# Both gates' first 512 columns computed as one Strassen unit of seven block products between the q and k products

## The chip, the cores and the metric

The kernel runs on one core of a Trainium2 chip. Its time is the device time of one launch in microseconds (us), the median of several runs. The engines are TensorE (PE: matmul, with PEld for its weight loads), VectorE (DVE), ScalarE (ACT), GpSimd (POOL) and SyncE (SP), which issues most transfers. On-chip data lies in SBUF, and matmuls write to banks of PSUM.

## The reference

Two layers, each with a feed-forward part, a mixer and a second feed-forward part, with layer norms between them. There are 256 tokens and 1024 channels, all in float32. The change is in the mixer:

```python
def _mixer(x, layer, w_in, gate_b, ...):
    z = x @ w_in                                   # 256 x 1024 times 1024 x 7168
    u, v, q, k, val, gates = jnp.split(z, SPLITS, axis=-1)
    ...
    q = _rope(q, cos, sin)                         # rotary
    k = _rope(k, cos, sin)
    o = _diff_attention(q, k, val, lam_full)       # 8 heads
    ...
    g = jax.nn.sigmoid(gates.reshape(bsz, seq, N_BRANCH, D_MODEL) + gate_b)
    m = g[:, :, 0] * (h_a @ w_branch[0]) + g[:, :, 1] * (h_b @ w_branch[1])
    return m @ w_out
```

`gates` is x times 2048 columns: 1024 for each of the two branches. The change is about the first 512 columns of each branch, so a product of 256 x 1024 with 1024 x 1024.

## The kernel before, in words

Float32 products are made of three matmuls. Each weight is split into a high part (`hi`, ScalarE, `activation Copy`, lines 195 and 247) and a low part (`lo`, VectorE, a subtraction, lines 197 and 249), x likewise, and a product is hi by hi, lo by hi and hi by lo. A weight arrives as a tile `raw` of 128 x 2048 floats, 1 MB, by a transfer that SP issues (`fetch`, line 173). Four such tiles are there, and eight halves each of `hi` and `lo`. So weights are fetched and split up to four tiles ahead of TensorE. A new fetch into a `raw` waits until VectorE has made the low parts of its old content.

Two forms of product stand in the mixer. `gemm_a2` takes weights as the stationary side: 16 matmuls of 128x512 (line 295) and 16 of 128x256 (line 302). ScalarE copies one half of the bank to `r` (line 303) and VectorE adds the other half into z (lines 305, 307). `gemm_b` takes x as the stationary side, with matmuls of 128x512 in line 283. `product`, with its matmul in line 376, is one block of a Strassen product as the feed-forward parts use them: 12 matmuls of 128x512. `gather` (line 353) adds a second weight onto a `raw` in place, by two accumulating transfers of 512 KB that GpSimd issues. `pieces` splits a raw into its high and low halves. `strassen_sums` makes four sums of blocks of x on VectorE and splits them.

The order on TensorE is the order of the code. The other engines' instructions are ordered ahead of the run by a scheduler that takes the code's order as priority. `beat` counts TensorE's work in units of 12 matmuls of 128x512. `beside(task, n)` lets a task's steps run n such units later, among the products. `behind(ins)` keeps an instruction behind another one on its engine.

A mixer runs as follows:

- `val`, two column blocks by `gemm_b2`.
- Four pairs of heads `hp`. For each a q product and a k product by `rope`, which multiplies z with the cosine on VectorE (line 992), swaps halves of z by two transfers on SP (line 989), multiplies the swapped half with the sine on GpSimd (line 993) and adds both on VectorE (line 997). Then `attend(hp)` as a task, 4.5 + 2.1 hp units later: scores (line 1017), masked copies with maxima on VectorE (line 1029), exponentials on ScalarE (line 1031), the difference of both maps on VectorE (lines 1048, 1049, 1040), copies on GpSimd (line 216), transposing transfers on SP (line 220), and the product with `val` (lines 1071, 1073).
- For each branch `gate_rows`, 48 matmuls in line 283 for 512 gate columns with VectorE's addition of the bias (line 1125) and a tanh on ScalarE, and `gate_columns`, two `gemm_a2` for the other 512 columns.
- Then u, v, the branch products, the output product and the norm.

`Norm` computes a layer norm in pieces and leaves x and its transposed blocks `rows`; the norm with `front` 0 is the one ahead of a mixer.

Of the kernel before, what the change touches and what calls it, by code (L numbers as in the profile page):

```python
# [17 lines left out]
ALU = mybir.AluOpType  # L18
# [36 lines left out]
def trunk(ctx, tc, x, xT, w13a, w13b, w2, wb, wqk, wu, wg, wgr, wbr, wbrr, wo, gateb, gatebr, sgug, sgub, sguwT, sgubias, lam, diffg,  # L55
# [538 lines left out]
    class Norm:  # L594
# [25 lines left out]

        def halved(self):
            with behind(line[0]):
                A.activation(self.g, self.g, AF.Copy, scale=-0.5)
            yield 0
# [30 lines left out]
        def finish(self, t, waits):  # L655
# [3 lines left out]
            if not self.last:  # L659
                r = rsqrt(mv[:, 1:2], self.eps)  # L660
                halves = slice(0, 512), slice(512, D)
                if t:
                    self.via += [t512("nvia") for _ in halves]
# [7 lines left out]
                if t == 0:  # L671
                    self.via.append(s512("nvia"))
# [36 lines left out]
        def turned(self, wait):  # L709
# [5 lines left out]
            self.affine(0, 0, b, s512("xf"), (4,))  # L715
# [59 lines left out]
        def close(self):  # L775
# [3 lines left out]
            return self  # L779

    def ffn(l, f, i, norm, last=False):
# [77 lines left out]

        def strassen_sums(to, made, v11, v21, v12, v22, apart=1, after=lambda: None):  # L860
            to[:] = [tuple(lambda k, v=v: v[:, k * P : (k + 1) * P] for v in m) for m in made]
            for n, (out, a, b, op) in ((0, (v22, v21, v22, ALU.subtract)), (2, (v21, v11, v21, ALU.subtract)),
                                       (1, (v11, v22, v11, ALU.subtract)), (3, (v12, v12, v11, ALU.add))):
                with behind(after()):
                    V.tensor_tensor(out=out, in0=a, in1=b, op=op)
                if n in (2, 3):
                    yield apart
            for n, out in ((0, v22), (2, v21), (1, v11), (3, v12)):
                split(*(v if len(out.shape) == 2 else v.rearrange("p (k t) -> p k t", k=4) for v in made[n]), out)
                yield apart  # L870
# [98 lines left out]
    def mixer(l, i, norm):  # L969
# [139 lines left out]

        for hp in range(HEADS // 2):  # L1110
            qT = rope(wqk[l, hp, 0], HD ** -0.5)
            kT = rope(wqk[l, hp, 1], 1.0)
            beside(attend(hp, qT, kT), 4.5 + 2.1 * hp)
            if hp == 1:
                gbias = bc_load(gatebr[l], qT[:, :1])

        gates, grow = [], []

        def gate_rows(br):

            gr = [slots("gr", 2)[0] for _ in range(NT)]
            grow.append(gr)

            def done(t, ps, c, n):
                added[0] = V.tensor_tensor(out=gr[t], in0=ps, in1=gbias[:, br * 512 : (br + 1) * 512], op=ALU.add).ins
                emptied[0] = A.activation(gr[t], gr[t], AF.Tanh, scale=0.5).ins
# [231 lines left out]
```

## Time and profile before

| what | value |
|---|---|
| median of 3 runs | 1186.49 us (1186.29 to 1186.53) |
| span of the profiled execution | 1185.1 us |
| granted clock of TensorE | 1.000 |
| HBM read | 248.05 MB, 210 GB/s over the span |
| longest instruction group of VectorE | line 197, 346 times, 379.4 us |

The span is that of one execution under the profiler, from its first to its last instruction; the runs' times also hold what lies around it. Busy time of an engine is a sum over stages, so a stage is read from windows of it, and what an engine waited for from the waits. In a row of a timeline the first number is the start, the second the duration, and x the count of instructions joined in it; neighbours on one engine overlap a little, so costs are taken from start to start. Layer 0's q product begins at 202.44 us on TensorE, layer 1's at 788.67 us.

### The profile page before, as it was taken

The page shows a single profiled execution, that of the slowest core. Times are in us where ns is not written, and L with a number is a line of the kernel's source. Part 1 is how long each engine was busy: PE and PEld are TensorE (multiplying, and loading weights), DVE is VectorE, ACT ScalarE, POOL GpSimd, SP SyncE. Part 2 cuts the span into 40 slices and gives each one's busy share as a digit, 9 for nine tenths or more (in the row PEclk, how much of TensorE's full clock was granted, in tenths as well). Part 3 has the DMA queues.
Part 4 walks back from the last instruction along what each step waited for, and adds up shares of the span by engine and source line. Part 5 has one row for each costly group of instructions (what it writes and reads, how often), then busy time and mean ns, then how long its engine had stood idle before and what let it go on. Part 6 is the DMA issues. An engine that isn't in the chain of part 4 may idle for free.

```text
span 1185.1 us, 16676 instructions
## 1 busy us (share of the span) xinstructions
PE 1180.5 (100%) x5777; PEld 995.0 (84%) x5777; DVE 1013.1 (85%) x1562; ACT 828.1 (70%) x1419; POOL 287.5 (24%) x350
## 2 busy tenths in 40 slices
PE   9999999999999999999999999999999999999998
PEld 8888888888888888888888888888888888888887
DVE  6989989788688989889899889888965989988895
ACT  6688658559955677876667876576788556679761
POOL 1011201247420220051020161003564112102600
PEclk9999999999999999999999999999999999999999
DMA  9869976767865658699668689586666755786881
GB/s 355 265 198 262 287 273 208 266 193 238 246 205 173 227 188 273 187 275 267 239 220 265 190 278 280 198 290 232 212 204 208 250 181 174 247 254 208 273 260 36
DMA packets 129621, 275.10 MB, mean 232 GB/s; under 512 B 89041, under 2 KB 90369, under 8 KB 105473
## 3 DMA queue, kind: packets, MB, share of 16 engines
q1 hardware_dynamic: 121968, 248.67, 63.5%
q0 software_dynamic: 6992, 24.71, 8.7%
q8 instruction: 45, 0.74, 0.2%
q10 hardware_dynamic: 576, 0.66, 0.2%
q14 instruction: 40, 0.32, 0.1%
HBM read 248.05 MB, written 1.05 MB: 210 GB/s over the span
## 4 chain that ended last, share of the span: by engine, by line
PE 99%; DVE 0%; DVEq 0%; issue 0%
PE bank L283 46%; PE bank L295 15%; PE sbank L376 12%; PE bank L410 10%; PE bank L302 8%; PE sbank L410 3%; PE bank L530 2%; PE sbank L1017 1%; PE bank L376 1%; PE sbank L1073 1%; PE sbank L1191 1%; PE sbank L542 0%; PE sbank L1071 0%; PE sbank L714 0%; DVE xtok L701 0%; DVE st L643 0%
## 5 line engine op out<-in xcount | busy, mean ns | idle before, releaser
L197 DVE TENSOR_TENSOR wlo<-raw,whi 128x1024 fp32r<-128x1024 f32 (+1 forms) x346 | 379.4, 1123 | 51.8 <-ACT whi L195 38.0
L195 ACT ACTIVATE whi<-raw 128x1024 fp32r<-128x1024 f32 (+1 forms) x350 | 323.4, 952 | 135.1 <-PE bank L283 43.0
L283 PE MATMUL bank<-whi,x 128*128 128x512 f32 x1224 | 386.4, 390 | 0.0
L283 PEld LDWEIGHTS bank<-whi,x 128*128 128x128 f32 x1224 | 229.8, 188 | 47.8
L283 PE MATMUL bank<-wlo,x 128*128 128x512 f32 x612 | 238.2, 389 | 0.0
L249 DVE TENSOR_TENSOR wlo<-raw,whi 128x1024 fp32r<-128x1024 f32 (+1 forms) x123 | 142.9, 1185 | 20.3 <-ACT whi L247 11.4
L247 ACT ACTIVATE whi<-raw 128x1024 fp32r<-128x1024 f32 (+1 forms) x123 | 121.1, 1003 | 51.2 <-DVE raw L359 23.9
L295 PE MATMUL bank<-x,whi 128*128 128x512 f32 x640 | 153.3, 391 | 0.0
L295 PEld LDWEIGHTS bank<-x,whi 128*128 128x128 f32 x640 | 118.2, 188 | 23.8
L283 PEld LDWEIGHTS bank<-wlo,x 128*128 128x128 f32 x612 | 114.9, 188 | 23.1
L229 POOL COPY seven<-seven 128x512 uint16<-128x512 uint16 x16 | 58.8, 3733 | 135.2 <-ACT whi L195 54.6
L302 PEld LDWEIGHTS bank<-x,wlo 128*128 128x128 f32 x640 | 81.4, 191 | 2.9
L302 PE MATMUL bank<-x,wlo 128*128 128x256 f32 x640 | 82.6, 283 | 0.0
L410 PE MATMUL bank<-whi,hhi 128*128 128x512 f32 (+1 forms) x182 | 68.2, 374 | 0.0
L410 PE MATMUL bank<-whi,hlo 128*128 128x512 f32 (+1 forms) x182 | 67.9, 373 | 0.0
L410 PE MATMUL bank<-wlo,hhi 128*128 128x512 f32 (+1 forms) x182 | 67.9, 373 | 0.0
L993 POOL TENSOR_TENSOR swap<-swap,sin_t 128x512 f32<-128x512 f32 x16 | 26.9, 1680 | 101.2 <-DMA swap<-z 84.4
L757 POOL COPY nvia<-ntwo 128x256 uint16<-128x256 uint16 x20 | 10.0, 547 | 161.2 <-DMA ntwo<-nvia 148.2
L303 ACT ACTIVATE r<-bank 128x256 f32<-128x256 f32 x96 | 34.9, 373 | 16.3 <-PE bank L302 16.1
L376 PE MATMUL sbank<-whi,xhs 128*128 128x512 f32 x128 | 42.0, 389 | 0.0
L410 PEld LDWEIGHTS bank<-whi,hlo 128*128 128x128 f32 x182 | 34.3, 188 | 6.0
L410 PEld LDWEIGHTS bank<-whi,hhi 128*128 128x128 f32 x182 | 34.3, 188 | 6.0
(292 smaller groups left out, 2157.6 us busy)
## 6 DMA issues: line engine op xcount, KB each, us to landing
raw<-in_w13b SPq DMA_DIRECT2D x68, 1024.0 KB, 6.0
raw<-in_w SPq DMA_DIRECT2D x32, 1024.0 KB, 7.0
raw<-in_wb SPq DMA_DIRECT2D x16, 1024.0 KB, 6.7
raw<-in_wqk SPq DMA_DIRECT2D x16, 1024.0 KB, 6.2
home<-in_w13b SPq DMA_DIRECT2D x16, 512.0 KB, 5.9
raw<-in_w13a SPq DMA_DIRECT2D x8, 1024.0 KB, 4.9
home<-in_w SPq DMA_DIRECT2D x16, 512.0 KB, 4.9
raw<-in_wgr SPq DMA_DIRECT2D x8, 1024.0 KB, 5.4
```

What stands on the lines that cost most here:

```text
L195: inline(A, A.activation(h, r, AF.Copy).ins)
L197: low = eng.tensor_tensor(out=w, in0=r, in1=h.bitcast(F32), op=ALU.subtract).ins
L229: eng.tensor_copy(out=o, in_=i)
L247: a = A.activation(hi, src, AF.Copy).ins
L249: return a, eng.tensor_tensor(out=lo, in0=src, in1=hi.bitcast(F32), op=ALU.subtract).ins
L283: PE.matmul(ps, xx, w, start=start and n == 0, stop=stop and n == 2)
L295: PE.matmul(b[-1], hi[:, k * P : (k + 1) * P], xc(k), start=k == 0, stop=False)
L302: PE.matmul(b[n][:, :T], lo[:, k * P : (k + 1) * P], xc(k)[:, :T], start=False, stop=k == KT - 1)
L303: emptied[0] = A.activation(r[:, s], b[n][:, T:], AF.Copy, scale=scale).ins
L376: PE.matmul(ps, x[o](k), y, start=start and k == n == 0, stop=stop and k == 3 and n == 2, skip_group_check=True)
L410: PE.matmul(q[c][t][:, :n] if o == 0 else more[:, :n], x(k, t), y, start=k == 8 and m == 0 and (c, t) != (1, 0) and not o, stop=k == FT - ...
L993: turned_by[0] = G.tensor_tensor(out=s3, in0=s3, in1=s, op=ALU.mult).ins
```

## The change

Both branches' first 512 columns become one 2 x 2 block product: x in blocks of 128 tokens by 512 channels, weights in blocks of 512 channels by 512 columns, one column block for each branch. It is computed by seven block products P1 to P7 of 12 matmuls each in place of 96 matmuls. The blocks' weights w11, w21 and w22 are fetched; w12, and the sums that follow, come in by `gather`: r1 holds w11, then w11 + w12, then with w22 added, then with w21 added, and r3 holds w22, then w22 + w12. The bank `bz` serves P3 and P4, `bx` serves P1, P5, P6 and P7; VectorE copies the intermediate values out between. The four sums of x (`strassen_sums`, now outside `ffn`) are made by a task 2.5 units behind the start of the q and k products, into eight slots `xhs`.

The generator `gates_by_rows` is advanced by `next(products)`: behind k0 for P1, behind q1 for P2, and so on, so that TensorE has q0 k0 P1 q1 P2 k1 P3 q2 P4 k2 P5 q3 P6 k3 P7. An attend comes 4.5 + 0.1 hp units after its k. The gate bias is loaded ahead of the q products. The norm ahead of the mixer keeps some tiles in slots and no longer in temporary tiles (`home`), since they are read longer.

```diff
--- before.py
+++ after.py
@@ -618,6 +618,9 @@
                 self.via = []
                 self.x = [xs.tile([P, 4, 512], F32R, tag="x", name=name("x")) for _ in range(2)]
 
+        def home(self, s, other):
+            return other(s) if self.front else slots(s, 2)[0]
+
         def halved(self):
             with behind(line[0]):
                 A.activation(self.g, self.g, AF.Copy, scale=-0.5)
@@ -660,7 +663,7 @@
                 r = rsqrt(mv[:, 1:2], self.eps)
                 halves = slice(0, 512), slice(512, D)
                 if t:
-                    self.via += [t512("nvia") for _ in halves]
+                    self.via += [self.home("nvia", t512) for _ in halves]
                 for h in (0, 1) if t else (1, 0):
                     s = halves[h]
                     with behind(self.ends[t]):
@@ -669,7 +672,7 @@
                     if t:
                         self.ends[t] = self.plane(V, t, h, 1)
                 if t == 0:
-                    self.via.append(s512("nvia"))
+                    self.via.append(self.home("nvia", s512))
                     for w in range(2):
                         self.ends[t] = self.plane(V, 0, 1, w)
                     beside(self.turned(waits), 0)
@@ -712,7 +715,7 @@
             b = side_bank()
             for k in range(4):
                 PE.transpose(b[:, k * P : (k + 1) * P], self.y[0][:, k * P : (k + 1) * P], ident)
-            self.affine(0, 0, b, s512("xf"), (4,))
+            self.affine(0, 0, b, self.home("xf", s512), (4,))
             yield 9
             yield from self.tokens(0)
 
@@ -778,6 +781,18 @@
                 x_cat = self.x
             return self
 
+    def strassen_sums(to, made, v11, v21, v12, v22, apart=1, after=lambda: None):
+        to[:] = [tuple(lambda k, v=v: v[:, k * P : (k + 1) * P] for v in m) for m in made]
+        for n, (out, a, b, op) in ((0, (v22, v21, v22, ALU.subtract)), (2, (v21, v11, v21, ALU.subtract)),
+                                   (1, (v11, v22, v11, ALU.subtract)), (3, (v12, v12, v11, ALU.add))):
+            with behind(after()):
+                V.tensor_tensor(out=out, in0=a, in1=b, op=op)
+            if n in (2, 3):
+                yield apart
+        for n, out in ((0, v22), (2, v21), (1, v11), (3, v12)):
+            split(*(v if len(out.shape) == 2 else v.rearrange("p (k t) -> p k t", k=4) for v in made[n]), out)
+            yield apart
+
     def ffn(l, f, i, norm, last=False):
         xh, xl = parts(both)
         h_hi, h_lo = ([act.tile([P, 512], F32R, tag="slot", name=name(n)) for _ in range(FT // 2)] for n in ("hhi", "hlo"))
@@ -856,18 +871,6 @@
 
             made = [[home(v) for v in w] for w in (("main", "side"), ("side", "main"), ("main", "slot"), ("side", "slot"))]
             yield from strassen_sums(x_sums, made, t11, t21, t12, t22, after=lambda: None if norm else line[1])
-
-        def strassen_sums(to, made, v11, v21, v12, v22, apart=1, after=lambda: None):
...
 
         def seven(src, x_sums):
 
@@ -1107,25 +1110,68 @@
                     V.scalar_tensor_tensor(out=lo, in0=f, scalar=dl, in1=hi.bitcast(F32), op0=ALU.mult,
                                             op1=ALU.subtract)
 
+        gates, x_sums = [], []
+        grow = [[slots("gr", 2)[0] for _ in range(NT)] for _ in range(2)]
+        gbias = bc_load(gatebr[l], val[1][:, 1, :1])
+
+        def sums_of_x():
+            made = [slots("xhs", 4, F32R) for _ in range(4)]
+            t11, t12, t21, t22 = (norm.rows[v] for v in ((0, 0), (0, 1), (1, 0), (1, 1)))
+            yield from strassen_sums(x_sums, made, t11, t21, t12, t22, after=lambda: added[0])
+
+        def gates_by_rows():
+
+            x11, x12, x22 = (tuple(lambda k, o=o, t=t, h=h: x_cat[h][:, k, o + t * P : o + (t + 1) * P] for o in (0, T))
+                             for t, h in ((0, 0), (0, 1), (1, 1)))
+            (w11, w21), (w12, w22) = ([wgr[l, br, 0][:, o : o + CH] for o in (0, CH)] for br in range(2))
+            (g00, g10), (g01, g11) = grow
+            bias = [gbias[:, br * 512 : (br + 1) * 512] for br in range(2)]
+
+            def sum_up(out, in0, in1, op, end=False):
+                added[0] = V.tensor_tensor(out=out, in0=in0, in1=in1, op=op).ins
+                if end:
+                    emptied[0] = A.activation(out, out, AF.Tanh, scale=0.5).ins
+
+            bx = bank()
+            r1 = fetch(w11)
+            product(bx, x11, pieces(r1), True, False)
+            gather(r1, w12)
+            sum_up(g00, bx, bias[0], ALU.add)
+            yield
+            bq = bank()
+            product(bq, x12, pieces(fetch(w21)), True, True)
+            sum_up(g00, bq, g00, ALU.add, True)
+            yield
+            bz = bank()
+            product(bz, x_sums[0], pieces(r1), True, False)
+            gather(r1, w22)
+            sum_up(g11, bz, bias[1], ALU.add)
+            yield
+            r3 = fetch(w22)
+            product(bz, x_sums[3], pieces(r3), False, True)
+            gather(r3, w12)
+            sum_up(g01, bz, bias[1], ALU.add)
+            yield
+            product(bx, x_sums[1], pieces(r1), False, False)
+            gather(r1, w21)
+            sum_up(g01, g01, bx, ALU.subtract, True)
+            yield
+            product(bx, x_sums[2], pieces(r3), False, False)
+            sum_up(g11, g11, bx, ALU.subtract, True)
+            yield
+            product(bx, x22, pieces(r1), False, True)
+            sum_up(g10, bx, bias[0], ALU.add, True)
+            yield
+
+        products = gates_by_rows()
+        beside(sums_of_x(), 2.5)
         for hp in range(HEADS // 2):
             qT = rope(wqk[l, hp, 0], HD ** -0.5)
+            if hp:
+                next(products)
             kT = rope(wqk[l, hp, 1], 1.0)
-            beside(attend(hp, qT, kT), 4.5 + 2.1 * hp)
-            if hp == 1:
-                gbias = bc_load(gatebr[l], qT[:, :1])
-
-        gates, grow = [], []
-
-        def gate_rows(br):
-
-            gr = [slots("gr", 2)[0] for _ in range(NT)]
-            grow.append(gr)
-
-            def done(t, ps, c, n):
-                added[0] = V.tensor_tensor(out=gr[t], in0=ps, in1=gbias[:, br * 512 : (br + 1) * 512], op=ALU.add).ins
-                emptied[0] = A.activation(gr[t], gr[t], AF.Tanh, scale=0.5).ins
-
-            gemm_b(wgr[l, br, 0], KT, xh, xl, done, tail=TAIL)
+            beside(attend(hp, qT, kT), 4.5 + 0.1 * hp)
+            next(products)
 
         def gate_columns(br):
             gt = slots("gate", KT // 2)
@@ -1137,7 +1183,6 @@
                     A.activation(gt[c][:, s], b[:, s], AF.Tanh, scale=0.5, bias=gbh[:, l, br, k : k + 1])
 
         for br in range(2):
-            gate_rows(br)
             gate_columns(br)
 
         g_bc, b_bc = (bc_load(v[l], gates[0][0][:, :1]) for v in (sgug, sgub))
```

VectorE in layer 0, between the first attend's masked copies and its difference of maps. Before, with `whi` and `wlo` of `raw_2496` and `raw_2506` belonging to the first gate rows:

```order
L197 TENSOR_TENSOR wlo_2499<-raw_2496,whi_2498 128x1024
L307 SCALAR_TENSOR_TENSOR z_2233<-bank_2178,r_2232 128x256
L997 TENSOR_TENSOR qk_2160<-qk_2160,swap_2159 128x512
L307 SCALAR_TENSOR_TENSOR z_2233<-bank_2223,r_2232 128x256
L1048 RECIPROCAL rc_2190<-sums_2188 128x4
L197 TENSOR_TENSOR wlo_2503<-raw_2496,whi_2502 128x1024
L1049 SCALAR_TENSOR_TENSOR c_2189<-rc_2190,neg_lam_1894,sums_2188 128x4
L1040 SCALAR_TENSOR_TENSOR d_2257<-pp_2208,c_2189,pp_2203 128x256 x2
L1040 SCALAR_TENSOR_TENSOR d_2258<-pp_2218,c_2189,pp_2213 128x128 x2
L992 TENSOR_TENSOR qk_2265<-z_2233,cos_t 128x512
L197 TENSOR_TENSOR wlo_2509<-raw_2506,whi_2508 128x1024
```

And now, where `raw_2373` is r3, `raw_2398` k2's weight, `z_2252` belongs to k1, and the last row is the copy of P3's bank `bank_2288` into `gr_1939`:

```order
L249 TENSOR_TENSOR wlo_2376<-raw_2373,whi_2375 128x1024
L305 TENSOR_TENSOR z_2252<-bank_2194,r_2251 128x256
L249 TENSOR_TENSOR wlo_2380<-raw_2373,whi_2379 128x1024
L305 TENSOR_TENSOR z_2252<-bank_2242,r_2251 128x256
L1051 RECIPROCAL rc_2208<-sums_2206 128x4
L197 TENSOR_TENSOR wlo_2401<-raw_2398,whi_2400 128x1024
L1052 SCALAR_TENSOR_TENSOR c_2207<-rc_2208,neg_lam_1894,sums_2206 128x4
L197 TENSOR_TENSOR wlo_2405<-raw_2398,whi_2404 128x1024
L1043 SCALAR_TENSOR_TENSOR d_2275<-pp_2226,c_2207,pp_2221 128x256 x2
L1043 SCALAR_TENSOR_TENSOR d_2276<-pp_2236,c_2207,pp_2231 128x128 x2
L995 TENSOR_TENSOR qk_2283<-z_2252,cos_t 128x512
L1131 TENSOR_TENSOR gr_1939<-bank_2288,bc_1940 128x512
```

The difference of maps and the cosine product stood in the same place before; four low parts stand ahead of them now where two did, and the copy of P3 follows them.

TensorE, from q2's low parts to k2. Before:

```order
L302 MATMUL bank_2280<-x_1212,wlo_2273 128x256 x4
L302 MATMUL bank_2280<-x_1213,wlo_2273 128x256 x4
L302 MATMUL bank_2289<-x_1212,wlo_2277 128x256 x4
L302 MATMUL bank_2289<-x_1213,wlo_2277 128x256 x4
L295 MATMUL bank_2341<-x_1212,whi_2333 128x512 x4
L295 MATMUL bank_2341<-x_1213,whi_2333 128x512 x4
```

And now, with `bank_2288` the bank that P3 has left and P4 goes on in; its 12 matmuls are in line 376, of which the first three are shown:

```order
L302 MATMUL bank_2322<-x_1212,wlo_2315 128x256 x4
L302 MATMUL bank_2322<-x_1213,wlo_2315 128x256 x4
L302 MATMUL bank_2332<-x_1212,wlo_2319 128x256 x4
L302 MATMUL bank_2332<-x_1213,wlo_2319 128x256 x4
L376 MATMUL bank_2288<-whi_2375,xhs_2024 128x512
L376 MATMUL bank_2288<-wlo_2376,xhs_2024 128x512
L376 MATMUL bank_2288<-whi_2375,xhs_2025 128x512
```

The first row of line 376 begins P4, which adds onto `bank_2288`, so it follows VectorE's copy of that bank.

GpSimd from the end of the norm to the first attend's copies. Before (line 993 is the sine product):

```order
L993 TENSOR_TENSOR swap_1986<-swap_1986,sin_t 128x512
L993 TENSOR_TENSOR swap_2045<-swap_2045,sin_t 128x512
L993 TENSOR_TENSOR swap_2102<-swap_2102,sin_t 128x512
L591 DMA bc_2165<-in_gatebr 128x1024
L993 TENSOR_TENSOR swap_2159<-swap_2159,sin_t 128x512
L993 TENSOR_TENSOR swap_2264<-swap_2264,sin_t 128x512
L216 COPY d_2258<-d_2258 128x256 x2
L216 COPY aT_2259<-d_2257 128x512 x2
```

And now (line 353 is the gather, line 996 the sine product):

```order
L353 DMA raw_2071<-in_wgr 128x1024 x2
L591 DMA bc_1940<-in_gatebr 128x1024
L996 TENSOR_TENSOR swap_1993<-swap_1993,sin_t 128x512
L353 DMA raw_2071<-in_wgr 128x1024
L996 TENSOR_TENSOR swap_2064<-swap_2064,sin_t 128x512
L353 DMA raw_2071<-in_wgr 128x1024
L996 TENSOR_TENSOR swap_2151<-swap_2151,sin_t 128x512
L353 DMA raw_2373<-in_wgr 128x1024 x2
L996 TENSOR_TENSOR swap_2282<-swap_2282,sin_t 128x512
L216 COPY d_2276<-d_2276 128x256 x2
L216 COPY aT_2277<-d_2275 128x512 x2
```

A gather stands ahead of each of the first four sine products, and the bias load `bc` ahead of all of them.

More of the change, by code (lines that the diff above doesn't have):

```diff
@@ L858, in sums_of_x @@
             yield from strassen_sums(x_sums, made, t11, t21, t12, t22, after=lambda: None if norm else line[1])
-        def strassen_sums(to, made, v11, v21, v12, v22, apart=1, after=lambda: None):
[L861 to L870, printed above, removed]
         def seven(src, x_sums):
```

## The prediction

> **What bounds the kernel now.** First the page: busy shares, and the chain of work that ended last.
>
> ```profile
> PE 1180.5 (100%) x5777; PEld 995.0 (84%) x5777; DVE 1013.1 (85%) x1562; ACT 828.1 (70%) x1419; POOL 287.5 (24%) x350
> ...
> PE 99%; DVE 0%; DVEq 0%; issue 0%
> ```
>
> The chain is TensorE almost alone. Then the waits of TensorE, to see whether it ever stands still:
>
> ```profile
> PE sbank L542 <- DVE warm L538: 1.0, 1, 1.0
> PE sbank L693 <- ACT minus L691: 0.2, 1, 0.2
> ```
>
> Two waits, 1.2 us in all, and neither is near a mixer. So a matmul that is taken away is worth its whole issue time, as long as no other engine comes late for what is left. Issue time is read from the chain in order of time, not from the mean duration of one, which overlaps the next:
>
> ```profile
> 202.44 3.63 PE bank L295 x16
> 206.07 1.91 PE bank L302 x16
> 207.98 3.65 PE bank L295 x16
> ...
> 224.68 1.84 PE bank L295 x8
> 226.52 1.51 PE sbank L1017 x16
> ...
> 275.49 5.47 PE bank L283 x24
> 280.96 0.22 PE sbank L1071 x2
> ...
> 282.30 2.73 PE bank L283 x12
> ```
>
> A q or k product is 3.63 + 1.91 = 5.54 to 5.57 us; I use 5.56. With an attend's 16 scores in its middle it ran from 224.68 to 231.98, where the next row of 16 begins: 7.30 us. Twelve matmuls of 128x512 take 2.73 us and 24 take 5.47, so 0.227 each. The output of one attend (280.96 to 282.30) is 1.3 us.
>
> Next, how much room VectorE has. These windows cover layer 0's q/k products (207 to 262) and the first gate products behind them; the columns after the sum are busy PE, PEld, DVE, ACT, POOL, the clock, the DMA share and GB/s:
>
> ```profile
> 207.00:219.00 12.00, 12.00 (x74) 10.71 (x73) 9.09 (x13) 6.02 (x10) 1.73 (x2) 1.00 0.90 339
> 219.00:235.00 16.00, 16.00 (x95) 13.65 (x95) 12.86 (x35) 9.80 (x27) 5.21 (x4) 1.00 0.66 231
> 235.00:247.00 12.00, 12.00 (x78) 10.34 (x77) 10.36 (x17) 6.15 (x9) 6.09 (x5) 1.00 0.51 153
> 247.00:262.00 15.00, 15.00 (x81) 12.96 (x80) 11.17 (x32) 7.38 (x25) 4.05 (x3) 1.00 0.66 218
> ```
>
> In 55 us of products VectorE works 9.09 + 12.86 + 10.36 + 11.17 = 43.5. It is free for 11.5 us, but early on only, while it waits for rotary swaps. The granted clock is 1.00 throughout.
>
> **The change, part by part.** *Removed from TensorE.* Per layer 96 matmuls become 84, so 12 x 0.227 = 2.72 us, and 5.44 us over both layers. All have the shape of the quoted rows. Without a new wait the time is 1186.49 - 5.44 = 1181.05. The profiled span is 1185.1, which is 1.4 us under the median of the runs; I take that difference as unchanged.
>
> *Added to VectorE.* Seven products per layer need 14 halves of low parts where four weights needed 8. There are seven evacuations where there were four, some with a second one for a shared bank's next use, and eight operations of 128x512 on row sums of x. More weighty is the place: the weight splits and evacuations that stood behind the q/k stage now stand in it. Prices come from VectorE's timeline, start to start:
>
> ```profile
> 202.86 5.76 DVE L197 TENSOR_TENSOR wlo<-raw,whi 128x1024 fp32r<-128x1024 f32 x5
> 208.54 0.75 DVE L307 SCALAR_TENSOR_TENSOR z<-bank,r 128x256 f32<-128x256 f32 x2
> 209.20 1.22 DVE L197 TENSOR_TENSOR wlo<-raw,whi 128x1024 fp32r<-128x1024 f32 x1
> ...
> 216.90 0.69 DVE L997 TENSOR_TENSOR qk<-qk,swap 128x512 f32<-128x512 f32 x1 [1.19 <-POOL swap L993]
> 217.51 0.68 DVE L992 TENSOR_TENSOR qk<-z,cos_t 128x512 f32<-128x512 f32 x1
> ...
> 228.97 0.42 DVE L1029 CUSTOM_DVE_ANT_0 pp<-sbank,mask 128x256 f32<-128x256 f32 x1
> ...
> 231.19 1.22 DVE L197 TENSOR_TENSOR wlo<-raw,whi 128x1024 fp32r<-128x1024 f32 x1
> ...
> 234.91 0.17 DVE L1048 RECIPROCAL rc<-sums 128x4 f32<-128x4 f32 x1
> 234.99 1.19 DVE L197 TENSOR_TENSOR wlo<-raw,whi 128x1024 fp32r<-128x1024 f32 x1
> 236.10 0.22 DVE L1049 SCALAR_TENSOR_TENSOR c<-rc,neg_lam,sums 128x4 f32<-128x4 f32 x1
> 236.36 1.41 DVE L1040 SCALAR_TENSOR_TENSOR d<-pp,c,pp 128x256 f32<-128x256 f32 x4
> 237.68 0.68 DVE L992 TENSOR_TENSOR qk<-z,cos_t 128x512 f32<-128x512 f32 x1
> ```
>
> A low half: 5.68/5 = 1.135. A z evacuation: 0.66/2 = 0.33. A 128x512 operation: 217.51 - 216.90 = 0.61. An attend's masked copies: 231.19 - 228.97 = 2.2. Its scaling: 0.08 + 0.26 + 1.32 = 1.7.
>
> *The wait it adds.* P4 accumulates in the bank that P3 leaves, so P4's first matmul waits for VectorE's copy of P3. VectorE works in order. Between the rotary add of q0 and the end of that copy stand 9 low halves (10.2), 13 operations of 128x512 (7.9), 5 z evacuations (1.7), one attend's copies (2.2) and its scaling (1.7): 23.7 us. The add is a fixed point, since it waits for the swap's way through SP, a transfer and GpSimd. In layer 0 it ended at 217.51. The copy then ends at 217.5 + 23.7 = 241.2. TensorE wants P4 after q0, k0, q1, q2 (4 x 5.56), k1 with scores (7.30) and P1 to P3 (3 x 2.72): 37.7 us behind 202.44, at 240.1. **TensorE waits 1.1 us in layer 0.** What is queued behind the copy on VectorE is the next rotary add and the splits for P5; they shift with TensorE, which stands too. In layer 1:
>
> ```profile
> 788.67 3.79 PE L295 MATMUL bank<-x,whi 128*128 128x512 f32 x16
> ...
> 800.26 1.29 POOL L993 TENSOR_TENSOR swap<-swap,sin_t 128x512 f32<-128x512 f32 x1 [22.68 <-DMA swap<-z]
> ```
>
> The swap is multiplied by 801.55, so the add ends at 802.2 and the copy at 825.9. P4 is due at 788.67 + 37.7 = 826.4: no wait, 0.5 us to spare.
>
> The next tight place is the second half of the first gate-column product, which needs the bank of k3. From P3's copy to k3's evacuation VectorE has 16 low halves (18.2), 10 operations of 128x512 (6.1), 8 z evacuations (2.7), two attends' copies (4.4) and one scaling (1.7): 33.1 us. TensorE has P4 to P7 (10.9), k2 and k3 with scores (14.6), q3 (5.56), one output (1.3) and a first half of 1.84: 34.2. That leaves 1.1 us to spare in layer 0 and 1.6 in layer 1.
>
> *What GpSimd does to VectorE.* The attend's copies on GpSimd now run beside a VectorE that has no spare time:
>
> ```profile
> 240.60 1.20 POOL L216 COPY d<-d 128x256 uint16<-128x256 uint16 x2
> 241.75 2.16 POOL L216 COPY aT<-d 128x512 uint16<-128x512 uint16 x2
> ```
>
> ```profile
> 240.69 0.85 DVE L997 TENSOR_TENSOR qk<-qk,swap 128x512 f32<-128x512 f32 x1 [0.85 <-POOL swap L993]
> ...
> 241.80 1.64 DVE L197 TENSOR_TENSOR wlo<-raw,whi 128x1024 fp32r<-128x1024 f32 x1
> 243.36 1.09 DVE L992 TENSOR_TENSOR qk<-z,cos_t 128x512 f32<-128x512 f32 x1
> ```
>
> Beside them the add took 0.85 against 0.69, the split 1.64 against 1.22 and the product 1.09 against 0.69: 1.0 us in all. One such stretch begins just ahead of P3's copy, a second one ahead of k3's evacuation. So between 0 and 2.0 us per layer is added to VectorE, of which the room above takes 1.1 to 1.6. I take 0.7 us of stall in layer 0 beside the 1.1, and 0.5 us in layer 1: together **2.3 us, within 1.1 and 3.9**.
>
> In the Trainium skill, "SBUF — State Buffer", section "Who interferes with whom", a VectorE instruction with two SBUF inputs and a GpSimd instruction that reads SBUF exclude each other, and the one that comes later stands until the other is done. The trace agrees only in part: beside 3.4 us of copies VectorE lost 1.0 us, not 3.4. By the rule the three swap multiplications and the copies ahead of P3's copy could cost up to 7.3 us per layer, from the rows 1.29 and 3.4.
>
> *The gathers.* Eight accumulating transfers per layer are issued by GpSimd. The nearest rows are the existing ones of the feed-forward parts (min, median, max):
>
> ```profile
> L353 POOL DMA_DIRECT2D raw<-in_w13b x6: 850/870/917, 474.2 to 1061.8; - x6
> ...
> DMA to landing us min/median/max: 5.6/9.4/11.4
> ```
>
> The first pair waits for the low halves of r1, the second and third of the five splits from 202.86, so until 206.3; with 0.87 for each issue they are under way at 208.0 and land at 217.4, at worst at 219.4. ScalarE's high half takes 1 us more. VectorE comes to that split at 217.51 + 2.7 = 220.2, so 1.8 us later in the median. I cost the wait at nothing; its upper end is the second rival. The swap multiplications queued behind the gathers on GpSimd wait for them in turn: k0's is done near 223.5, and VectorE asks for it near 224.3.
>
> *At nothing.* The norm's other tiles, the earlier bias load and the attend's earlier start change places, not work on TensorE; they lie beside matmuls that have no waits. ScalarE gains the high halves but was idle for about half of the q/k windows (29.4 of 55 us busy). At both ends: below zero is excluded, since TensorE has no wait to lose there; above, they would lengthen the VectorE sum by at most one 0.61 operation each.
>
> **The forecast.** 1181.05 + 2.3 = 1183.35, say 1183.4 us. Its own range is 1182.1 to 1185.0.
>
> **Rivals.** *Full saving.* Over the whole stage the work would fit: 43.5 us plus 14 halves (15.9), seven copies (4.3) and the sums (4.9) is 68.6 of 55 + 19 = 74. If q0's swap lands as in the median of all swaps, the wait at the add goes:
>
> ```profile
> swap<-z SPq DMA_DIRECT2D x32, 128.0 KB, 2.1
> ```
>
> For the first swap of layer 0 it was more: issued from 209.31, it was there at 215.54.
>
> ```profile
> 209.31 1.17 SPq L989 DMA_DIRECT2D swap<-z  x2
> ...
> 215.54 1.32 POOL L993 TENSOR_TENSOR swap<-swap,sin_t 128x512 f32<-128x512 f32 x1 [24.74 <-DMA swap<-z]
> ```
>
> With 1.1 us less, no stall remains: 1181.1 to 1182.1.
>
> *Gathers late.* If the first pair lands 3 us later than the worst row, VectorE stands 3 us ahead of P3, and the stall is 4.0 in layer 0 and 2.5 in layer 1: 1187.5. Against it speaks that other gathers met queues as full.
>
> *Slower: the swap lands behind the new transfers.* The first swap is issued while the first gathers are under way and the DMA share is 0.90. If it takes the gathers' 9.4 us instead of 6.2 (209.31 to 215.54), the fixed point moves by 3.2, and the stall is 1.1 + 3.2 + 0.7 = 5.0 in layer 0 and, with 0.5 to spare, 2.7 + 0.5 = 3.2 in layer 1: 1181.05 + 8.2 = 1189.3. The point: above 5.44 us of stall together nothing is gained, and above 7.8 it is slower beyond measuring error.
>
> *The lock in full.* With 7.3 us on VectorE ahead of P3's copy the stalls are 8.4 and 6.8: 1196.3. The rows beside the copies speak against it.
>
> *It doesn't do what it says:* the count of matmuls stays; 1186.5.
>
> **How the numbers follow.** A measurement of this kernel can tell about 0.2%, 2.4 us, from no change, so faster ends at 1184.1 and slower begins at 1188.9. Forecast 0.45 (0.30 faster, 0.15 same); full saving 0.22, faster; gathers late 0.08, same; swap late 0.18 (0.10 slower, 0.08 same); the lock 0.04, slower; no change in matmuls 0.03, same. Together faster 0.52, same 0.34, slower 0.14. From 1181.0 to 1188.8 the range leaves out only the slow part of the last cases.
>
> **What would show it.** PE's count falls by 24, to 5753. P4 should wait for VectorE's copy of P3 by about 1 us in layer 0, hardly in layer 1, and the gate-column product by under 1 us. q0's rotary add should end near 217.5, with TensorE's q0 at 202.4. If VectorE waits long for a split behind a gather, the second rival holds; if the add ends after 219, the third. I am wrong if another engine, ScalarE above all, holds back TensorE in this stage, or if the norm ahead of the mixer is late.

## The result, and the profile after

The changed kernel takes 1249.99 us (median of 4 runs, 1247.47 to 1252.13) against 1186.51 us before: 1.053 times, 95% interval 1.052 to 1.055. It is 63 us slower where 3 us less were forecast. The page of the profiled execution, whose span is 1247.6 us, begins so:

```profile
PE 1196.3 (96%) x5753; PEld 1001.9 (80%) x5753; DVE 1038.2 (83%) x1596; ACT 842.4 (68%) x1439; POOL 279.3 (22%) x366
...
PE 82%; DVE 7%; DMA 7%; POOL 1%; issue 1%; ACT 1%; SPq 0%; DVEq 0%; POOLq 0%; ACTq 0%
```

The 24 matmuls are gone, so the change does what it says. But TensorE is 1247.6 - 1196.3 = 51.3 us without work, where it was 4.6 before, and it is busy longer with fewer matmuls. 1180.5 - 5.4 = 1175.1 us were due, 1196.3 were used: 21.2 us more. The sum is closed: 46.7 us more without work + 21.2 us more at work - 5.4 us saved = 62.5 us, the difference of the spans.

Where TensorE waits (line, releaser, us in total, times, longest):

```profile
PE bank L295 <- DVE z L305: 20.7, 5, 5.9
PE bank L283 <- ACT lhi L195: 13.4, 2, 6.7
PE bank L295 <- DVE z L307: 11.1, 4, 3.5
```

There are two places in each layer. One lies ahead of the mixer, where val's first matmuls wait for ScalarE's `lhi`. The other is the q/k stage, where a product waits for a bank that VectorE has not yet emptied (lines 305 and 307). A wait for P3's copy (line 1131) is not among them. The granted clock (the column ahead of the DMA share) is low where TensorE waits and 1.00 where it doesn't:

```profile
177.00:190.00 13.00, 6.01 (x23) 4.17 (x22) 11.94 (x28) 10.23 (x22) 2.86 (x4) 0.79 0.50 142
...
275.00:290.00 15.00, 11.19 (x53) 9.76 (x54) 13.81 (x30) 13.27 (x31) 5.72 (x5) 0.77 0.44 159
...
330.00:350.00 20.00, 20.00 (x117) 17.66 (x117) 12.74 (x20) 19.54 (x45) 9.13 (x21) 1.00 0.85 240
```

**The place ahead of the mixer.** ScalarE before, in its timeline:

```profile
160.63 1.13 ACT L195 ACTIVATE lhi<-raw 128x512 fp32r<-128x512 f32 x2
...
164.68 1.66 ACT L195 ACTIVATE lhi<-raw 128x512 fp32r<-128x512 f32 x3
```

And SP's queue before, where q0's weight is fetched:

```profile
166.32 0.33 SPq L173 DMA_DIRECT2D raw<-in_wqk  x1
```

ScalarE, TensorE and SP after, from three timelines:

```profile
171.85 1.15 ACT L195 ACTIVATE whi<-raw 128x512 fp32r<-128x512 f32 x2 [8.05 <-PE bank L410]
...
186.50 0.61 ACT L195 ACTIVATE lhi<-raw 128x512 fp32r<-128x512 f32 x1
...
187.97 1.65 ACT L195 ACTIVATE lhi<-raw 128x512 fp32r<-128x512 f32 x3
```

```profile
187.17 0.80 PE L283 MATMUL bank<-lhi,x 128*128 128x512 f32 x1 [6.70 <-ACT lhi L195]
```

```profile
179.55 0.33 SPq L173 DMA_DIRECT2D raw<-in_wqk  x1
```

`lhi` and `llo` are halves of val's weights that are lent to the 26 slots of `act`. Before, they were made from 160.6 us on. Now the norm's four tiles hold slots, and `lhi` stands behind the norm in ScalarE's order. The time in which those halves were made goes unused: ScalarE idles for 8.05 us ahead of 171.85, where it idled for 5.56 at the same place before. The raw tiles of val come free later, so q0's weight is fetched at 179.55 and no longer at 166.32, and q0 begins at 211.66 in place of 202.44.

**The q/k stage.** The rotary swap, from the DMA issues, and VectorE's waits:

```profile
swap<-z SPq DMA_DIRECT2D x32, 128.0 KB, 5.4
```

```profile
DVE qk L1000 <- POOL swap L996: 43.6, 13, 8.8
```

The swap's median landing was 2.1 us and is now 5.4, and VectorE waits 43.6 us for swaps where it waited 8.6 in eight times before:

```profile
DVE qk L997 <- POOL swap L993: 8.6, 8, 3.1
```

One such wait, in the timelines of SP, GpSimd, VectorE and TensorE:

```profile
263.97 1.81 SPq L992 DMA_DIRECT2D swap<-z  x2
```

```profile
271.92 1.28 POOL L996 TENSOR_TENSOR swap<-swap,sin_t 128x512 f32<-128x512 f32 x1 [9.58 <-DMA swap<-z]
```

```profile
273.24 0.69 DVE L1000 TENSOR_TENSOR qk<-qk,swap 128x512 f32<-128x512 f32 x1 [8.82 <-POOL swap L996]
...
278.34 0.42 DVE L305 TENSOR_TENSOR z<-bank,r 128x256 f32<-128x256 f32 x1
```

```profile
278.81 3.78 PE L295 MATMUL bank<-x,whi 128*128 128x512 f32 x8 [5.89 <-DVE z L305]
```

VectorE stands 8.8 us at the add. Behind it in order stand masked copies, splits and the evacuation of z, for which TensorE waits. When TensorE goes on, 8 matmuls take 3.78 us, where the 8 from 270.95 took 1.98 in the same view. So the loss is a loop: evacuation, swap, sine product, add, and only then the next evacuation.

Part of this wait is not the swap's own way. Its z was ready at 259.50, and SP issued the swap 4.5 us later, behind two transposing transfers of an attend:

```profile
259.90 1.25 SPq L220 DMA_TRANSPOSE d<-aT  x1
261.25 2.62 SPq L220 DMA_TRANSPOSE d<-d  x1
```

Four of the 16 swaps in the changed kernel are issued 3.4 to 4.5 us behind their z in this way, one before (3.4 us). No run tried this place alone.

### The profile page after: what moved, and what is told of

The parts are those of the page before. It is cut to its first block, busy times and chain, and to the rows that moved or that the text cites. A ratio compares the mean times of both kernels' runs of the same rounds, so it can differ in the third digit from the quotient of the medians.

```text
span 1247.6 us, 16730 instructions
## 1 busy us (share of the span) xinstructions
PE 1196.3 (96%) x5753; PEld 1001.9 (80%) x5753; DVE 1038.2 (83%) x1596; ACT 842.4 (68%) x1439; POOL 279.3 (22%) x366
## 4 chain that ended last, share of the span: by engine, by line
PE 82%; DVE 7%; DMA 7%; POOL 1%; issue 1%; ACT 1%; SPq 0%; DVEq 0%; POOLq 0%; ACTq 0%
PE bank L283 40%; PE sbank L376 11%; PE bank L295 10%; PE bank L410 8%; PE bank L302 5%; DMA swap<-z 5%; PE sbank L410 3%; PE bank L530 2%; DVE wlo L249 2%; DVE wlo L197 2%; POOL swap L996 1%; PE bank L376 1%; DVE qk L1000 1%; DMA raw<-in_wgr 1%; PE sbank L1236 1%
## 5 line engine op out<-in xcount | busy, mean ns | idle before, releaser
L195 ACT ACTIVATE whi<-raw 128x1024 fp32r<-128x1024 f32 (+1 forms) x334 | 307.1, 947 | 149.0 <-PE bank L283 48.1
L197 DVE TENSOR_TENSOR wlo<-raw,whi 128x1024 fp32r<-128x1024 f32 (+1 forms) x330 | 355.5, 1103 | 60.6 <-ACT whi L195 50.5
L283 PE MATMUL bank<-whi,x 128*128 128x512 f32 x1096 | 344.4, 389 | 0.0
L283 PEld LDWEIGHTS bank<-whi,x 128*128 128x128 f32 x1096 | 205.8, 188 | 42.6
L283 PE MATMUL bank<-wlo,x 128*128 128x512 f32 x548 | 213.2, 389 | 0.0
L295 PE MATMUL bank<-x,whi 128*128 128x512 f32 x640 | 165.6, 413 | 31.8 <-DVE z L305 20.7
L249 DVE TENSOR_TENSOR wlo<-raw,whi 128x1024 fp32r<-128x1024 f32 (+1 forms) x151 | 177.7, 1199 | 21.0 <-ACT whi L247 10.1
L247 ACT ACTIVATE whi<-raw 128x1024 fp32r<-128x1024 f32 (+1 forms) x151 | 149.9, 1012 | 58.4 <-DVE raw L359 24.6
L283 PEld LDWEIGHTS bank<-wlo,x 128*128 128x128 f32 x548 | 102.9, 188 | 21.3
L283 PE MATMUL bank<-lhi,x 128*128 128x512 f32 x120 | 41.7, 416 | 13.5 <-ACT lhi L195 13.4
L1000 DVE TENSOR_TENSOR qk<-qk,swap 128x512 f32<-128x512 f32 x16 | 12.9, 804 | 43.8 <-POOL swap L996 43.6
L1034 ACT ACTIVATE pp<-pp,mx 128x256 f32<-128x256 f32 (+1 forms) x64 | 28.2, 441 | 29.7 <-DVE mx L1032 29.7
```

What stands on the lines that cost most here:

```text
L195: inline(A, A.activation(h, r, AF.Copy).ins)
L197: low = eng.tensor_tensor(out=w, in0=r, in1=h.bitcast(F32), op=ALU.subtract).ins
L247: a = A.activation(hi, src, AF.Copy).ins
L249: return a, eng.tensor_tensor(out=lo, in0=src, in1=hi.bitcast(F32), op=ALU.subtract).ins
L283: PE.matmul(ps, xx, w, start=start and n == 0, stop=stop and n == 2)
L295: PE.matmul(b[-1], hi[:, k * P : (k + 1) * P], xc(k), start=k == 0, stop=False)
```

## The experiments

Two theories stood at first. N: the norm's slots spoil the start, and the stage stalls because its weights come late. S: the strung stage stalls by itself, at adds that wait for swaps. Each of the first twelve kernels ran once, beside the kernel before, which took 1186.3 to 1186.8 us. The kernels with long waits that ran four times spread by 4.5 to 6.1 us, so differences of that size between single runs are not told apart.

**The norm's part alone**, on the kernel before:

```diff
+        def home(self, s, other):
+            return other(s) if self.front else slots(s, 2)[0]
...
-                    self.via += [t512("nvia") for _ in halves]
+                    self.via += [self.home("nvia", t512) for _ in halves]
...
```

> The kernel before with one part of the change alone: the norm ahead of the mixer keeps its tiles in slots. Theory N (the norm's four slots make val's lent weight halves wait, the weights behind them are fetched late, and the q/k stage starts without its lead): TensorE waits 6 to 7 us for lhi ahead of each val, and also stands in the q/k stage; 1200 to 1215 us. Theory S (the strung q/k stage stalls by itself, at rotary adds that wait for swaps): the wait ahead of val is there, 9 us per layer with the lower clock, but no wait of TensorE behind it; 1203 to 1206 us. If the norm's edit is free, 1186.5.

Measured: 1208.2 us. TensorE's only new wait above 1 us is the one for `lhi`:

```profile
PE bank L283 <- ACT lhi L195: 14.6, 2, 7.8
```

So the edit costs 21 us without any other part of the change. The time lies in N's range and 2 us above S's, but the stage behind val does not stall, which speaks for S in the q/k stage. TensorE's busy time was 1186.8, 6.3 us above before, with a granted clock of 0.992.

**The same without lent weights.** In val's product `lent` is empty for the norm with front 0, so no weight goes to slots:

```diff
-            lent = [(0, 1), (0,), (), ()]
+            lent = [(), (), (), ()] if norm.front == 0 else [(0, 1), (0,), (), ()]
```

> home_alone, with val's weights ahead of the mixer split into the rings of high and low halves only, none into slots. If the wait for slots is what the norm's edit costs, TensorE's 14.6 us of waits for lhi go and the time falls from 1208 to under 1197 us. If the norm itself is late, TensorE waits as long for other rows there, and the time stays at 1203 us or more.

Measured: 1190.6 us, with no wait for a high half left. The norm is not late by itself. The wait for slots is 17.6 of the edit's 21.4 us; the other 3.8 stay open, since the kernel before was not run without lent weights.

**The norm's tiles as before, and the sums of x right behind val**, in the changed kernel:

```diff
-            return other(s) if self.front else slots(s, 2)[0]
+            return other(s)
...
-            yield from strassen_sums(x_sums, made, t11, t21, t12, t22, after=lambda: added[0])
+            yield from strassen_sums(x_sums, made, t11, t21, t12, t22, apart=0.2)
...
-        beside(sums_of_x(), 2.5)
+        beside(sums_of_x(), 0)
```

> The changed kernel with the norm's tiles back in temporary tiles, and the sums of x made right behind val. N: the waits for lhi are gone and with them most of the waits in the q/k stage; 1182 to 1195 us. S: only the 9 us per layer ahead of q0 go, VectorE still waits some 40 us for swaps; 1228 to 1235 us.

Measured: 1226.3 us, 23.7 below the change, a little under S's range. This kernel, and all that build on it, also make the sums of x sooner and closer together, so the 23.7 us are not the norm's tiles alone. VectorE still waited 41.6 us for swaps. N falls as the cause of the stage's stall; its own loss is real.

**Later rotary adds** in the changed kernel:

```diff
-            beside(rest(), 1.55)
+            beside(rest(), 3.2)
```

> The changed kernel with each rotary add 3.2 units behind its product in place of 1.55, so that VectorE comes to it later in its order. S with the add as the place where VectorE loses its time: its waits for swaps fall from 43.6 us to under 20, and the time falls by 15 us or more, to about 1230 us. If the add is only where a lack of weights shows, the waits move to other rows and the time changes by less than 5 us.

Measured: 1220.4 us, 29.6 below. VectorE's waits for swaps fell from 43.6 to 11.5 us, though the swaps landed no sooner (6.2 us). This shows that the place of the add in VectorE's order makes the loop. A new wait comes up, 8.3 us in two times: P6 waits for VectorE's copy of P5.

**Both**, the two edits above in one kernel:

> norm_back and late_add together: the norm's tiles temporary again, and each rotary add 3.2 units behind its product. If the two losses are separate, they add: 1250 - 23 - 29 = 1198 us, with no wait for lhi and a few us of waits for VectorE. If a start with weights at hand and a late add mend the stage as a whole, 1181 to 1187 us. If both mend the same loss, 1215 us or more.

Measured: 1206.7 us. The two losses overlap by some 10 us; none of the three numbers was met. The wait for P5's copy is there again. It is of the kind that the prediction had looked for at P4, but at P6 (its 12 matmuls, then attend's output, follow the wait at 268.05):

```profile
PE bank L376 <- DVE gr L1131: 9.8, 2, 5.1
```

In layer 0 that copy stands behind q2's rotary add, where VectorE waits 3.79 us for a swap that SP issued 6.8 us after its z was ready. So the loop is still there, later in the order.

**norm_back without gathers:**

```diff
             product(bx, x11, pieces(r1), True, False)
-            gather(r1, w12)
```

and so for all four.

> norm_back without the eight accumulating transfers per layer: the block products use w11, w21 and w22 unsummed, so the gates are others. If the gathers make the swaps late (their bytes beside the swaps, and their place ahead of the sine products on GpSimd), the swaps' median landing falls from 5.8 us to 2 or 3 and the time from 1226 to under 1200 us. If the swaps are late because of the 1 MB fetches, landing stays at 5 us or more and the time above 1215 us.

Measured: 1208.1 us, 18.2 below norm_back; the swaps landed in 3.0 us and VectorE's waits for them fell from 41.6 to 17.0. The landing is as the first theory said, the time not quite. The edit also frees GpSimd of the issues, and the block products of the wait for a landing, so it does not show which of these counts. Beside both, the same edit is worth 16.9 us (1206.7 to 1189.8 in the run after next): the later add does not take away what the gathers cost.

**The same bytes by plain transfers** in place of accumulating ones, still issued by GpSimd:

```diff
+    def over(raw, more):
+        step()
+        for j, v in enumerate(halved(raw)):
+            G.dma_start(v, more[:, j * HC : (j + 1) * HC])
+        return raw
...
-            gather(r1, w12)
+            over(r1, w12)
...
```

and so for all four; the feed-forward parts keep their gathers.

> norm_back with plain transfers of the same bytes by GpSimd in place of the accumulating ones (the block products use unsummed weights, so the gates are others). If the accumulation itself makes the swaps late, their median landing falls from 5.8 to about 3 us and the time to about 1208 us, as without the gathers. If it is the bytes beside them and the place on GpSimd, landing stays above 5 us and the time near 1226 us.

Measured: 1212.4 us, swaps 4.8 us: the time is near the first theory's, the landing near the second's. GpSimd's queue in the three kernels (packets, MB, share of 16 engines over the span), norm_back, no_gather and this one:

```profile
q0 software_dynamic: 9296, 33.10, 12.4%
```

```profile
q0 software_dynamic: 6992, 24.71, 8.4%
```

```profile
q0 software_dynamic: 9296, 33.10, 10.6%
```

The 8.39 MB of gathers took 12.4% of 1224.6 less 8.4% of 1206.4, so 50.5 us of all 16 engines, when they accumulate, and 27.0 us when they don't. So 14 of the 18 us go with the accumulation; the 4 us left for the bytes and the place are within the spread of single runs. The swaps' median landing does not carry this alone: it fell by 1.0 of 2.8 us. VectorE's waits for swaps fell from 41.6 to 26.8 us, and the transfers onto r1 and r3 themselves landed in 5.1 in place of 7.0 us.

**All three mended**, both without the gathers:

> both without the eight accumulating transfers per layer (the block products use w11, w21 and w22 unsummed, so the gates are others). If slots, gathers and the early add are the whole loss, the time is 1181 to 1185 us and TensorE waits under 3 us. If VectorE's own work in the stage is too much (the theory of the prediction's tally: 1 to 2 us per layer), 1184 to 1190 us, with waits for copies of P banks and no idle time of VectorE ahead of them.

Measured: 1189.8 us, at the top of the second theory's range. TensorE is idle for 9.8 us, 5.2 more than before, and busy for 3.2 us more than due, at a granted clock of 1.000. Of its new waits, 3.6 us are for VectorE's evacuations and copies, none above 1.1 us, and 1.2 us for ScalarE and GpSimd. VectorE (the third busy time in this row) has no free time in the stage even with no gather at all, where before it worked 48.5 of the same 60 us:

```profile
202.00:262.00 60.00, 59.26 (x327) 49.82 (x326) 60.00 (x109) 42.05 (x83) 17.95 (x11) 1.00 0.60 203
```

**The products in one piece behind k3:**

```diff
-            if hp:
-                next(products)
...
-            next(products)
+        for _ in products:
+            pass
```

> The changed kernel with the seven products behind the last k product in one piece, in place of strung between. S: the waits at rotary adds go back to those of before (under 10 us) and the time is 1181 plus 18 for the norm's part, 1196 to 1203 us. N: the lost lead still stalls the q/k stage; 1215 us or more.

Measured: 1253.6 us, where neither theory had it:

```profile
PE bank L376 <- DVE gr L1131: 40.5, 6, 22.1
```

Six of the 14 block products wait for a copy. The longest wait, 22.14 us in layer 0, ends at 295.18 when P4 gets the bank of P3, whose matmuls had ended at 273.04. VectorE's copy of that bank stands in its order behind the last rotary add, and VectorE stood at this add for 10.18 us:

```profile
289.46 0.69 DVE L1000 TENSOR_TENSOR qk<-qk,swap 128x512 f32<-128x512 f32 x1 [10.18 <-POOL swap L996]
...
294.45 0.68 DVE L1131 TENSOR_TENSOR gr<-bank,bc 128x512 f32<-128x512 f32 x1
```

That swap was issued at 277.27, right behind two gathers. So the waits at adds went to 23.3 us, not under 10, since the first gathers still meet the last swaps. In layer 1 the same product waits 11.10 us without a wait at the add; there the copy stands behind masked copies, splits and the difference of maps. The run does not tell N from S by its time; its longest wait is S's add, with the copy of P3 behind it.

**Half the density**, from norm_back: no `next(products)` behind q products, one behind each pair of gate-column products and one behind u:

```diff
-            if hp:
-                next(products)
...
             gate_columns(br)
+            next(products)
...
         u_part((0, 1))
+        next(products)
```

> norm_back with the products spread out: one behind each k product (P1 to P4), one behind each pair of gate-column products (P5, P6) and one behind the first two u products (P7). If the stage loses because too much stands in it (gathers beside swaps, VectorE's work), half the density takes most of it away: 1181 to 1195 us. If each gather and swap costs its own wait wherever it stands, 1210 us or more.

Measured: 1238.4 us, 12 above norm_back and in the second theory's range; waits for swaps 31.2 us. And with the adds at 3.2:

> sparse with each rotary add 3.2 units behind its product. If waits for swaps remain in sparse, it is 5 to 10 us below sparse; if VectorE had time enough there, within 2 us of it.

Measured: 1231.4 us, 7 below, hardly more than the spread of single runs. Its chain through a wait of 5.2 us at a gate-column product runs through a late fetch:

```profile
297.97 7.13 DMA raw<-in_wu
305.12 1.06 ACT whi L195
...
309.99 1.22 DVE wlo L197
...
311.59 3.78 PE bank L295 x8
```

By the code r1 and r3 hold two of the four raw tiles for longer here, so weights are fetched with less lead. That this is why sparse is worse is read from this chain, not tried alone.

**Still later adds**, on norm_back: q's at 5.0, k's at 4.2 units:

```diff
-        def rope(src, scale):
+        def rope(src, scale, late):
...
-            beside(rest(), 1.55)
+            beside(rest(), late)
...
-            qT = rope(wqk[l, hp, 0], HD ** -0.5)
+            qT = rope(wqk[l, hp, 0], HD ** -0.5, 5.0)
...
-            kT = rope(wqk[l, hp, 1], 1.0)
+            kT = rope(wqk[l, hp, 1], 1.0, 4.2)
```

> norm_back with q's rotary add 5.0 and k's 4.2 units behind their products. If VectorE's remaining idle time at the adds (19.4 us in both) is what is left, 1190 to 1198 us. If VectorE's own work and the gathers hold it, 1203 us or more, with waits for copies of P banks.

Measured: 1201.7 us, between the two. The waits left are not at P banks but ahead of scores:

```profile
PE sbank L1020 <- DVE qk L1000: 12.9, 5, 5.5
```

**Later attends**, so that these adds have time, on later_add:

```diff
-            kT = rope(wqk[l, hp, 1], 1.0, 4.2)
-            beside(attend(hp, qT, kT), 4.5 + 0.1 * hp)
+            kT = rope(wqk[l, hp, 1], 1.0, (5.6, 5.6, 4.4, 4.2)[hp])
+            beside(attend(hp, qT, kT), (6.5, 6.5, 5.0, 4.6)[hp])
```

In late_attend_even the attend's delay is `6.5 - 0.5 * hp`. These two ran four times.

> later_add with the attends 6.5, 6.5, 5.0 and 4.6 units behind their k products, and k's rotary adds 5.6, 5.6, 4.4 and 4.2 units behind. In later_add TensorE still waited 12.9 us for k's adds ahead of scores, nearly all for the first two pairs. If that is all that is left beside the clock (PE's busy time was 5 us above its share), 1181 to 1186 us. If VectorE's own work is too much, its waits turn up at copies of P banks and z, and the time stays above 1192 us.

> The same with the attends 6.5, 6.0, 5.5 and 5.0 units behind. As late_attend if only the first two pairs matter; better than it by some us if the last two also wait for their adds; worse if attends that come later push their work into the gate columns, where TensorE then waits for VectorE.

Measured: 1207.9 us (1.017 of before, 1.015 to 1.019) and 1206.1 us (1.017, 1.015 to 1.018). The times stayed above 1192 us, as the second theory said, but the waits are not at P banks. It got no better than later_add, and the waits ahead of scores moved on, to later pairs: in late_attend the profile puts 8.1 us down to VectorE's one-column copy of a gate (line 590) and 7.6 us to adds, in late_attend_even 10.7 us to adds. The two versions are within each other's spread. So these delays did not hide what is left.

No version of the change beat the kernel before. The nearest that computes the whole, later_add, is 15 us above it.

## Why the prediction was wrong, point by point

- **The matmuls removed** were right in count, 24. Their 5.44 us were not seen by themselves: in both_no_gather, at a granted clock of 1.000, TensorE's busy time is 2.2 us below before (1178.3 against 1180.5), and the other 3.2 us are not explained.
- **"At nothing. The norm's other tiles ... change places, not work on TensorE"** was the first step that failed. home_alone shows 21.4 us. The step asked what work the tiles add and not who else draws on the slots; val's lent weights did, and their lateness moved the fetch of q0 by 13 us as well.
- **"The add is a fixed point"** was the second. For q0 it held: its add ended at 227.0, 15.4 us behind q0's start in layer 0, where 15.1 were forecast. But the sum let every later add find its swap there. In fact the swaps' median landing was 5.4 us, 13 of the 16 adds waited, 43.6 us in all, 38.6 of it from k1 on. The slow rival had the mechanism, a swap behind the new transfers. But it charged it once per layer, to q0, and came to 1189.3 us. It was mis-sized because in VectorE's order each later product can meet the delay again. late_add shows the loop (29.6 us); no_gather and plain_gather point to the gathers, and of them to the accumulation, as its driver (18.2 and 13.9 us). The swaps that wait on SP behind transposing transfers had no term either.
- **The price of a gather** was taken from its landing (9.4 us in the median, in fact 7.0 here). The DMA engines' time that the gathers take, 50 us for 8.39 MB, had no term; without them norm_back is 18.2 us faster. The rival with late gathers also left out the 0.7 and 0.5 us for GpSimd's copies that the forecast has; with them it would be about 1188.8 us, not 1187.5.
- **TensorE's wait for P3's copy** was put at 1.1 us. In the changed kernel it does not occur, but not because the copy was in time: it ended at 252.3, 40.7 us behind q0's start, where 38.8 were forecast, and TensorE had been held up by 2.2 us at k1. The wait shows once other things move, at P6 in late_add and both, at P4 in unstrung. As a statement on VectorE's work the sum was of the right kind: both_no_gather, with the other causes gone, waits 3.6 us for VectorE where 2.3 were forecast. That the sizes are so near is partly luck, since its adds stand later than in the sum. The full-saving rival's room, 68.6 of 74 us, was not there: VectorE worked 60.0 of 60 us.
- **The rows' clock.** All sums used matmuls at full rate. The waits had a second price: with 46.7 us more idle time came 21.2 us of slower matmuls.
- **GpSimd's copies beside VectorE** were priced from rows. In the changed kernel, splits beside them took 1.41 and 1.52 us against 1.22, much as before, so the forecast's rows held. But "the trace agrees only in part" is too hard on the lock, the rule of the Trainium skill, "SBUF — State Buffer", section "Who interferes with whom". It held all copies in a row against VectorE; a split that stands only for the rest of the copy under way loses no more than these 0.2 to 0.3 us. Where GpSimd comes later, its rows show the rule: a sine product that begins beside two splits (they end at 286.35) ends 1.2 us behind the second and takes 3.22 us, where the median is 1.29:

```profile
283.99 2.36 DVE L249 TENSOR_TENSOR wlo<-raw,whi 128x1024 fp32r<-128x1024 f32 x2
```

```profile
284.28 3.22 POOL L996 TENSOR_TENSOR swap<-swap,sin_t 128x512 f32<-128x512 f32 x1 [11.07 <-DMA swap<-z]
```

Not settled: how the last 15 us of later_add divide between late swaps and VectorE's work, since each edit that hid one moved waits to the other.

## What to carry to other kernels

Before an edit that "only" moves tiles to another pool is priced at nothing, list everything that draws on that pool near it: a slot that comes free later delays a split, the split delays a fetch, and the lead is gone. Where a transfer's result is awaited in an in-order queue between two evacuations, its latency can be paid at every product; place the consumer late in the queue. And a tightly packed TensorE has no use for fewer matmuls if the work that replaces them stands on an engine without free time in that stage.

## What the runs showed of the hardware

- **A stall can slow what follows, by where it falls.** In nearly all runs TensorE's busy time rose with its idle time; over before it was 6.3 us for 15 us more idle time in home_alone, 21.2 for 46.7 in the change. Two waits of nearly the same length in the changed kernel differ: behind one 8 matmuls take 3.59 us, behind the other 2.11 (1.98 without a wait):

```profile
236.02 3.59 PE L295 MATMUL bank<-x,whi 128*128 128x512 f32 x8 [2.23 <-DVE z L307]
...
854.73 2.11 PE L295 MATMUL bank<-x,whi 128*128 128x512 f32 x8 [2.20 <-DVE z L307]
```

  The trace's record of the granted clock tells them apart. Up to the end of the kernel half rate comes there only in stretches of 3.41 and 6.83 us, on a grid of 3.41 us. The first wait lies whole in one window of the grid (232.43 to 235.85, TensorE busy for 0.40 of it), and the next window has half rate; the second spreads over two windows (busy for 0.67 and 0.69). In the 15 traces behind the change taken together, each of the 61 windows at full rate with TensorE busy for 0.40 or less was followed by half rate, none of 147 partly idle ones above 0.45, and 6 of the 11 between. In the changed kernel 51.2 us have half rate and TensorE works in 38.9 of them, so half of these, 19.4 us, are the clock's part of the 21.2. The Trainium skill, "TensorE: Matmul & The Clock Gate", Part 1 on the clock gate, has the clock halved after an idle window of about 3.4 us; the length agrees with 3.41, but here a window idle for 0.6 of its length was enough.
- **Accumulating transfers occupy the DMA engines 1.9 times as long** as plain ones of the same bytes (50.5 against 27.0 us, with one run of each), and small transfers beside them land later (5.8 against 4.8 us in the median; 3.0 us with neither).
